# A fused two-block transformer kernel: sums moved to VectorE, a weight-difference loop in half the ticks, squares of one product set apart, a gate evacuation in parts

## The chip, the cores and the metric

The kernel runs on one core of one Trainium2 chip. A core has TensorE (PE, with its weight loads shown as PEld), VectorE (DVE), ScalarE (ACT), GpSimd (POOL) and SyncE (SP), which here issues all DMAs from one queue, in order. The metric is the device time of one execution in microseconds (us); lower is better.

## The reference, cut to what matters

A sequence of 1024 tokens of width 1024, in float32, passes through two blocks.

```python
# first block: dilated attention + RWKV-7 scan, merged by gates
h = rms_norm(x); proj = h @ w_in
y_attn = (o_attn * silu(z_attn)) @ w_up_attn
y_rwkv = (o_rwkv * silu(z_rwkv)) @ w_up_rwkv
merged = sigmoid(g_attn) * y_attn + sigmoid(g_rwkv) * y_rwkv
x = x + rms_norm(merged @ w_out)
# second block, first layer: gated spatial unit, 128-token chunks
u, v, z = split(rms_norm_2(x) @ a_w_in, 3)           # width 2048 each
s = W_causal @ layer_norm(gelu(v)) + b               # per chunk and group
x = x + rms_norm_2((gelu(u) * s * silu(z)) @ a_w_out)
# second block, second layer: sliding-window attention, 16 heads, 4 KV heads
q, z = split(rms_norm_2(x) @ b_w_in, 2)
out = x + rms_norm_2((attention(q, k, v) * silu(z)) @ b_w_out)
```

## The kernel before, in words

**Matmuls.** Every large product is made in three: weights and activations are split into a rounded high part (ACT: `whi`, `y_hi`, `Ahi`) and the rest (DVE: `wlo`, `y_lo`, `Alo`), and hi x hi, hi x lo and lo x hi are added up in a PSUM bank of 128 x 512. PSUM has two banks in pool `pd` and six in `pb`. SBUF tiles come from rings of slots: S2 (30 tiles of 128 x 512), S4 (19 of 128 x 1024) and A (8 of 128 x 2048). A slot goes to a new tile when the instructions and transfers of the old one are done; an instruction that writes the new tile waits for that.

**Order.** The order on each engine is the order in which the program emits instructions. Emission goes by ticks: `tick` (L166) is called after every four large matmuls and at the end of a group. A tick counts down the stores in `self.late` and issues those at the head of this list that are due (`store(dst, src, n)`, L157: n ticks later, four if nothing is said; the list is first in, first out), then loads and splits weights (`w_step`), then lets each lane go one step. A lane is a queue of generators; `yield n` means that the next part comes n ticks later. A `Bag` (such as `lane_n`) runs its generators side by side, a `Lane` one after the other. SP carries out its issues in the order of emission and stands still at a store whose source is not ready, so it runs ahead of the other engines until something holds it.

**Stages, in us of the profiled execution.** Up to 850: projections, and the RWKV scan beside them. 850 to 1160: dilated attention beside the rest of the projections (`phase1a`); in it `out_weights` (L1633) loads the four quadrants of a_w_out in eight row blocks, forms four differences on POOL (`minus`, tiles `tw`) and stores them in DRAM (`TW`). To 1440: the merge (`phase2`: gates loaded from `GT`, DVE's `m`) and the output product. 1440 to 1900: the second block's first layer (`phase3`): v, then for each of 16 column blocks the z and u products by a scheme of seven products (`seven`), with `vg` loaded for the spatial product. There `sums` (L2283) forms sums and differences of `y` that the output product wants, and stores them in `Y7`. 1913 to 2075: the output product a_out, itself in seven products (`run7`, L1976), each of four token tiles j; products n = 0 to 6, the sixth is n = 5. From the first half's results `norm` (L1935) makes residual, store of X2 and the next layer's normalised input, which PE transposes (`psT`). 2075 to 2505: the sliding-window attention (`phase4`) between projections, and the last output product. In `phase4` every z group is evacuated by `ev_z` (L2473): tanh on ACT, two products on DVE, the copy to `yb` on ACT, the difference on DVE. `att_norm` (L1092) divides the probabilities `P` on DVE before PE transposes them (L1122).

Of the kernel before, what the change touches and what calls it, by code (L numbers as in the profile page):

```python
# [9 lines left out]
F32 = mybir.dt.float32  # L10
F32R = mybir.dt.float32r
I32 = mybir.dt.int32
AF = mybir.ActivationFunctionType
# [1293 lines left out]
class Kernel(Attn):  # L1307
# [325 lines left out]
    def out_weights(self):  # L1633

        nc = self.nc
        W = self.I["a_w_out_2"][0]

        def load(r, c, k):
            t = self.s2("tw")
            nc.sync.dma_start(t, W[1024 * r + 128 * k:1024 * r + 128 * k + 128, 512 * c:512 * c + 512])  # L1640
            return t

        def minus(x, y, to, n, k):
            nc.gpsimd.tensor_tensor(out=to, in0=x, in1=y, op=ALU.subtract)
            if n is not None:
                self.store(self.TW[n][k], to, 4)

        for k in range(8):
            b11, b12, b22 = load(0, 0, k), load(0, 1, k), load(1, 1, k)
            yield 10  # L1650
            minus(b12, b11, b11, 0, k)
            yield 2
            minus(b22, b12, b12, 2, k)
            b21 = load(1, 0, k)
            yield 2
            minus(b22, b11, b22, 1, k)
            yield 6
            minus(b21, b22, b21, 3, k)
            yield 5

    def phase1a(self):
        self.att_setup()

        self.rw_pump(lambda: not self.lane_f.gens)
        self.lane_a.add(self.att_begin())
        self.lane_t = Lane(2)
        self.lane_a.add(self.att_tw())
        self.lanes = self.rw_lanes() + [self.lane_a, self.lane_m, self.lane_t]
        act = self.act_f
        i0 = self.first["pa"]  # L1670
        unit = lambda p, g: dict(p=p, g=g, L=T // DILATIONS[g], end=self.att_end1)
        A = self.lane_a
        us = {}

        def ahead(p, g):
            us[p, g] = unit(p, g)
            A.add(self.att_load(us[p, g]))

        def run(u):
            A.add(self.att_v(u))  # L1680
            A.add(self.att_unit(u))
        for n, x in enumerate(self.order_a):
            if type(x) is int:
                self.group(i0 + n, act, 8, 0, self.ev_g(self.GT[x - 57]))
                self.w_free(i0 + n)
                continue
            p, g, c = x
            dil = DILATIONS[g]
            if c == 2:
                while p > 1 and len(A.gens) > 7:  # L1690
                    for ln in self.lanes:
                        ln.step()
                u = unit(p, g)
            nm = ("q", "k", "vT")[c]
            u[nm] = self.s4(nm)
            ev = self.att_evac(u[nm], dil, 0.125 if c == 0 else None)
            for half in range(2):
                self.group(i0 + n, act, 8, half, ev)
            self.w_free(i0 + n)
            if c == 0:  # L1700
                u["bias"] = self.att_bias_load(g, p)
                ahead(p, 0)
                run(u)
                ahead(p, 1)
                run(us[p, 0])
                run(us[p, 1])
        self.lane_a.add(self.att_flush())
        i0 = self.first["pg"]
        self.gate_setup()
        for j, f in enumerate(self.order_g):  # L1710
            self.group(i0 + j, act, 8, 1, self.ev_g(self.GT[f - 57]))
            self.w_free(i0 + j)
# [145 lines left out]
    def out_proj(self, name, KT, post, xsrc, xdst, nxt, act):  # L1858
# [73 lines left out]
                nc.vector.scalar_tensor_tensor(out=x[:, s], in0=og[h], scalar=r, in1=x[:, s], op0=ALU.mult, op1=ALU.add)  # L1932
                nc.sync.dma_start(xdst[128 * tt:128 * tt + 128, s], x[:, s])

        def norm(half, og, x, ss, first=12, gap=3):  # L1935
            yield 2
            r = self.sm.tile([128, 4], F32, tag="or", name="or")
            st = self.sm.tile([128, 4], F32, tag="ost", name="ost")
            nc.vector.tensor_tensor(out=st, in0=ss[:, 0], in1=ss[:, 1], op=ALU.add)
            self.rms(st, r)  # L1940
            sv = self.sm.tile([128, 2, 4], F32, tag="osv", name="osv")
            for j in range(4):
                tt = 4 * half + j
                for h in range(2):
                    xs = x[j][:, 512 * h:512 * h + 512]
                    nc.vector.scalar_tensor_tensor(out=xs, in0=og[h, j], scalar=r[:, j:j + 1], in1=xs, op0=ALU.mult, op1=ALU.add)
                self.store(xdst[128 * tt:128 * tt + 128, :], x[j], 14 if nxt is not None else 0)
                yield 1
                if nxt is not None:
                    for h in range(2):  # L1950
                        nc.scalar.activation(out=og[h, j], in_=x[j][:, 512 * h:512 * h + 512], func=AF.Square,  # L1951
                                             accum_out=sv[:, h, j:j + 1])
            if nxt is None:
                return
            yield 2
            r2 = self.sm.tile([128, 4], F32, tag="or2", name="or2")
            nc.vector.tensor_tensor(out=st, in0=sv[:, 0], in1=sv[:, 1], op=ALU.add)
            self.rms(st, r2)

            def scaled(j):  # L1960
                for h in range(2):
                    xs = x[j][:, 512 * h:512 * h + 512]
                    if gnext is None:
                        nc.vector.tensor_scalar(out=og[h, j], in0=xs, scalar1=r2[:, j:j + 1], scalar2=None, op0=ALU.mult)
                    else:
                        nc.vector.scalar_tensor_tensor(out=og[h, j], in0=xs, scalar=r2[:, j:j + 1],
                                                       in1=gnext[:, 512 * h:512 * h + 512], op0=ALU.mult, op1=ALU.mult)
            scaled(0)
            for j in range(4):
                if j < 3:  # L1970
                    scaled(j + 1)
                yield gap if j else first
                yield from self.emit_T(lambda k: og[k // 4, j][:, 128 * (k % 4):128 * (k % 4) + 128], 4 * half + j, Ahi, Alo)
                self.act_done.add(4 * half + j)

        def run7(lanes, sums):  # L1976
# [24 lines left out]
            def evac(n, j, ps):  # L2001
                if n < 2:
                    t = (c1, c5)[n][j] = self.s2("og")
                    nc.scalar.copy(out=t, in_=ps)
                elif n == 2:
                    c2[j] = plus(ps, c1[j], self.s2("og"))
                elif n == 3:
                    out(0, 0, j, plus(ps, c1[j], c1[j]), nc.gpsimd)
                    u[j] = self.s2("og")
                    nc.gpsimd.tensor_tensor(out=u[j], in0=c2[j], in1=c5[j], op=add)  # L2010
                elif n == 4:
                    out(1, 0, j, plus(ps, u[j], u[j]), nc.vector)
                elif n == 5:
                    plus(ps, c2[j], c2[j])
                    nc.gpsimd.tensor_tensor(out=c5[j], in0=c2[j], in1=c5[j], op=add)
                    out(1, 1, j, c5[j], nc.gpsimd)
                else:
                    out(0, 1, j, plus(ps, c2[j], c2[j]), nc.vector)

            i0 = self.first[name]  # L2020
            for n in range(7):
# [20 lines left out]
                            evac(n, j, ps[j])  # L2042
                    self.w_free(i0 + 4 * n + kp)
                if n == 4:
                    self.lane_n.add(norm(0, og[0], x[0], ss[0], 18, 2))
            self.drain(self.lane_n)
            self.w_lim = 1000
            self.lane_n.add(norm(1, og[1], x[1], ss[1]))
# [178 lines left out]
    def phase3(self):  # L2227
# [55 lines left out]
        def sums(ct):  # L2283
# [2 lines left out]

            def do(x, y, op, n, to=None):
                t = self.s2("ysum") if to is None else to
                nc.gpsimd.tensor_tensor(out=t, in0=x, in1=y, op=op)
                self.store(self.Y7[n][c], t)  # L2290
                return t
            yield 4
            if ct < 8:
                do(ys[ct, 0], ys[ct, 1], ALU.subtract, 5)
                yield 2
# [129 lines left out]
    def phase4(self):  # L2425
# [38 lines left out]
                    self.group(self.first["bq"] + n, act, 8, 0, self.att_evac(qs[n], 1, 0.125))  # L2464
        self.Oh = {}
        yb = {}

        def end(u, Og):
            self.Oh[u["p"]] = Og

        def make_z(p):
            def ev_z(ps, half):
# [2 lines left out]
                s = slice(512 * half, 512 * half + 512)  # L2475
                t = self.s2("tz")
                nc.scalar.activation(out=t, in_=ps, func=AF.Tanh, scale=0.5)
                nc.vector.scalar_tensor_tensor(out=t, in0=t, scalar=1.0, in1=ps, op0=ALU.add, op1=ALU.mult)
                nc.vector.scalar_tensor_tensor(out=t, in0=t, scalar=0.5, in1=self.Oh[p][:, s], op0=ALU.mult, op1=ALU.mult)
                if p < 1:  # L2480
                    yb[p, half] = self.s2("yb_hi", F32R), self.s2("yb_lo", F32R)
                else:
                    y = self.s4("yb", F32R)
                    yb[p, half] = y[:, 0:512], y[:, 512:1024]
                self.split(t, *yb[p, half])
            return ev_z

        for n, c in enumerate(self.order_b):
            p = c % 8
# [5 lines left out]
            if c < 8:  # L2495
# [7 lines left out]
                self.lane_a.add(self.att_unit(u))  # L2503
                if p == 7:
                    self.lane_a.add(self.att_flush())
        self.flush()
        self.out3 = self.out_proj("b_out", 8, "b_post_g_2", self.X2, self.out, None, lambda k, half: yb[k, half])
        for half in range(2):
# [48 lines left out]
```

## Time and profile before

| | |
|---|---|
| median of 3 runs | 2505.64 us (2505.43 to 2506.14) |
| profiled execution | 2507.75 us, its span 2505.9 us |
| PE busy | 2418.4 us, 97% of the span |
| DVE, ACT, POOL busy | 1448.6, 1033.9, 832.8 us |
| mean granted clock of TensorE | 0.987 of full speed |

The span runs from the first to the last instruction. A matmul of 128 x 512 shows as some 0.39 us at full clock, but matmuls overlap, so PE's busy share counts time in which one was under way. A wait is put down to the instruction whose end released it.

### The profile page before, as it was taken

How to read it: one execution, taken by the hardware profiler on the slowest of the kernel's cores; microseconds unless marked ns; L12 is line 12 of the kernel's file. 1: busy time of each engine (PE TensorE's matmuls, PEld its weight loads, DVE VectorE, ACT ScalarE, POOL GpSimd, SP SyncE). 2: the span in 40 equal slices, each digit the busy share in tenths (PEclk: the TensorE clock that was granted, in tenths of full speed). 3: DMA queues.
4: the chain of work that ended last, by engine and by line, in shares of the span. 5: the costliest groups of instructions: out<-in, count | busy, mean ns of one | idle time of the engine just before them, and what ended most of it. 6: DMA issues, size and time to landing. Idle time of an engine off the chain costs nothing. (4 is left out here: it accounts for less than half of the span.)

```text
span 2505.9 us, 40000 instructions
## 1 busy us (share of the span) xinstructions
PE 2418.4 (97%) x14891; PEld 1904.7 (76%) x14891; DVE 1448.6 (58%) x3263; ACT 1033.9 (41%) x2539; POOL 832.8 (33%) x1055
## 2 busy tenths in 40 slices
PE   8999999999999999998899999999999988999998
PEld 6788777777777777776788778877777866777777
DVE  7764345554555355666747347556558666566545
ACT  4442232323232266553234223444445444566632
POOL 3443053434453012424500244656663122301000
PEclk8999999999999999999999999999999999999999
DMA  5334321212122346577733232333347743100033
GB/s 149 96 106 140 68 68 35 57 46 56 39 59 63 97 156 180 163 247 227 246 142 144 85 109 84 114 99 108 114 123 259 260 127 87 52 26 27 29 115 135
DMA packets 286263, 284.23 MB, mean 113 GB/s; under 512 B 27787, under 2 KB 208075, under 8 KB 286068
## 3 DMA queue, kind: packets, MB, share of 16 engines
q1 hardware_dynamic: 286068, 281.67, 36.3%
q8 instruction: 117, 1.92, 0.3%
q14 instruction: 78, 0.64, 0.1%
HBM read 206.87 MB, written 74.74 MB: 112 GB/s over the span
## 5 line engine op out<-in xcount | busy, mean ns | idle before, releaser
L349 PE MATMUL pd<-Ahi,whi 128*128 128x512 f32 x1232 | 497.4, 404 | 4.8 <-ACT whi L285 3.1
L349 PE MATMUL pd<-Ahi,wlo 128*128 128x512 f32 x1232 | 498.0, 404 | 4.0 <-DVE wlo L286 4.0
L349 PE MATMUL pd<-Alo,whi 128*128 128x512 f32 x1232 | 496.8, 403 | 1.4 <-DVE Alo L503 1.4
L286 DVE TENSOR_TENSOR wlo<-wraw,whi 128x512 fp32r<-128x512 f32 x348 | 279.6, 836 | 148.0 <-ACT whi L285 146.9
L349 PEld LDWEIGHTS pd<-Ahi,whi 128*128 128x128 f32 x1232 | 234.6, 190 | 57.7 <-ACT whi L285 3.7
L349 PEld LDWEIGHTS pd<-Alo,whi 128*128 128x128 f32 x1232 | 234.3, 190 | 55.1 <-issue 4.6
L349 PEld LDWEIGHTS pd<-Ahi,wlo 128*128 128x128 f32 x1232 | 234.3, 190 | 54.0 <-DVE wlo L286 5.8
L285 ACT ACTIVATE whi<-wraw 128x512 fp32r<-128x512 f32 x348 | 200.9, 621 | 36.9 <-DMA wraw<-in_b_w_out_dram 12.4
L1752 DVE TENSOR_TENSOR wlo<-wraw,whi 128x512 fp32r<-128x512 f32 x144 | 133.0, 934 | 81.1 <-ACT whi L1751 81.1
L1086 ACT ACTIVATE P<-P,ST 128x192 f32<-128x192 f32 (+2 forms) x320 | 130.5, 409 | 60.5 <-DVE ST L1074 57.3
L1751 ACT ACTIVATE whi<-wraw 128x512 fp32r<-128x512 f32 x144 | 89.5, 623 | 94.6 <-POOL wraw L228 91.7
L349 PE MATMUL pd<-wlo,Ahi 128*128 128x512 f32 x256 | 102.3, 400 | 5.2 <-DVE wlo L286 5.2
L799 POOL TENSOR_TENSOR X<-UC,X 128x60 f32<-128x60 f32 (+24 forms) x248 | 78.4, 316 | 82.8 <-DVE UC L792 64.4
L349 PE MATMUL pd<-whi,Ahi 128*128 128x512 f32 x256 | 101.4, 396 | 0.1
L349 PE MATMUL pd<-whi,Alo 128*128 128x512 f32 x256 | 101.3, 396 | 0.0
L228 POOL TENSOR_TENSOR wraw<-wraw 128x512 f32<-128x512 f32 x48 | 66.3, 1382 | 98.6 <-DVE wlo L1752 82.8
L278 POOL TENSOR_TENSOR wraw<-wraw,bpg 128x512 f32<-128x512 f32 x32 | 35.0, 1122 | 153.6 <-DMA wraw<-in_b_w_in_dram 141.5
L801 POOL TENSOR_TENSOR X<-X 128x60 f32<-128x60 f32 (+24 forms) x248 | 78.9, 318 | 19.4
L1157 PEld LDWEIGHTS psO<-PT,V 128*64 128x64 f32 x1040 | 55.6, 137 | 35.4 <-issue 18.2
L1157 PE MATMUL psO<-PT,V 128*64 128x128 f32 x1040 | 76.5, 284 | 5.1 <-DVE PT L1137 2.6
L1599 ACT ACTIVATE far<-pd 128x512 f32<-128x512 f32 x36 | 33.0, 917 | 101.9 <-PE pd L349 88.6
L2311 ACT ACTIVATE vg<-vg,lnv 128x128 f32<-128x128 f32 x128 | 53.4, 483 | 52.2 <-DMA vg<-Vd 51.7
(448 smaller groups left out, 5532.8 us busy)
## 6 DMA issues: line engine op xcount, KB each, us to landing
wraw<-in_w_in_dram SPq DMA_DIRECT2D x82, 512.0 KB
wraw<-in_a_w_in_dram SPq DMA_DIRECT2D x48, 512.0 KB
yraw<-Y SPq DMA_DIRECT2D x28, 512.0 KB
QD<-far SPq DMA_DIRECT2D x36, 256.0 KB
tw<-in_a_w_out_dram SPq DMA_DIRECT2D x32, 256.0 KB
TW<-tw SPq DMA_DIRECT2D x32, 256.0 KB
gate<-GT SPq DMA_DIRECT2D x32, 256.0 KB
wraw<-in_w_out_dram SPq DMA_DIRECT2D x16, 512.0 KB
```

Source lines behind the costliest of these rows:

```text
L228: nc.gpsimd.tensor_tensor(out=t[name], in0=t[x], in1=t[y], op=ALU.subtract)
L278: nc.gpsimd.tensor_tensor(out=t3[:, am], in0=t3[:, am], in1=gain[:, am].unsqueeze(2).to_broadcast([128, a // 2, b]), op=ALU.mult)
L285: nc.scalar.activation(out=his[j], in_=t[:, s], func=AF.Copy)
L286: nc.vector.tensor_tensor(out=los[j], in0=t[:, s], in1=his[j].bitcast(F32), op=ALU.subtract)
L349: nc.tensor.matmul(ps, lhsT=a, rhs=b, start=(n == 0), stop=(n == last))
L799: nc.gpsimd.tensor_tensor(out=tv, in0=U[:, j:j + 1, 0:j].to_broadcast([128, w, j]), in1=X[:, b0:8, j:j + 1].to_broadcast([128, w, j]), op= ...
L801: nc.gpsimd.tensor_tensor(out=X[:, b0:8, 0:j], in0=X[:, b0:8, 0:j], in1=tv, op=ALU.add)
L1086: nc.scalar.activation(out=it["P"][j][:, c], in_=Sx[j][:, c], func=AF.Exp, scale=-1.0, bias=ST[:, 0, n:n + 1], accum_out=ST[:, 1, n:n + 1])
L1157: nc.tensor.matmul(O(h).rearrange("p (s x) -> p s x", s=2), lhsT=V[:, b - 1 + t, c:c + 64], rhs=rhs, start=t == tiles[0], stop=t == 1)
L1751: nc.scalar.activation(out=hi, in_=src, func=AF.Copy)
L1752: nc.vector.tensor_tensor(out=lo, in0=src, in1=hi.bitcast(F32), op=ALU.subtract)
L2311: nc.scalar.activation(out=v[:, tt, :], in_=v[:, tt, :], func=AF.Identity, scale=lnv[:, tt, 1:2], bias=lnv[:, tt, 0:1])
```

## The change

Four places are changed. In `out_weights` all four loads of a row block come first, the subtractions follow at ticks 6, 7, 8 and 10, a block takes 12 ticks instead of 25, and a difference is stored 7 ticks after its subtraction instead of 4. `sums` works on VectorE instead of GpSimd, one tick sooner, and stores 8 ticks later instead of 4. In `run7` the squares (ACT) and scalings (GpSimd) of the sixth product leave its evacuation for a generator `last4`, which waits 6 ticks after the last tile and then does one tile per tick; the stores of X2 in the norm of the first half come 26 ticks after their sums instead of 14. In `phase4` the evacuation of a z group keeps only the tanh; the rest goes to a lane of its own in parts.

```diff
@@ out_weights
-                self.store(self.TW[n][k], to, 4)
+                self.store(self.TW[n][k], to, 7)
         for k in range(8):
             b11, b12, b22 = load(0, 0, k), load(0, 1, k), load(1, 1, k)
-            yield 10
+            b21 = load(1, 0, k)
+            yield 6
             minus(b12, b11, b11, 0, k)
+            yield 1
+            minus(b22, b12, b12, 2, k)
+            yield 1
+            minus(b22, b11, b22, 1, k)
             yield 2
-            minus(b22, b12, b12, 2, k)
-            b21 = load(1, 0, k)
+            minus(b21, b22, b21, 3, k)
             yield 2
-            minus(b22, b11, b22, 1, k)
-            yield 6
-            minus(b21, b22, b21, 3, k)
-            yield 5
@@ phase1a
-        self.lane_t = Lane(2)
+        self.lane_t = Lane(1)
@@ out_proj, norm
-        def norm(half, og, x, ss, first=12, gap=3):
+        def norm(half, og, x, ss, first=12, gap=3, late=14):
-                self.store(xdst[128 * tt:128 * tt + 128, :], x[j], 14 if nxt is not None else 0)
+                self.store(xdst[128 * tt:128 * tt + 128, :], x[j], late if nxt is not None else 0)
@@ out_proj, run7
                     nc.gpsimd.tensor_tensor(out=c5[j], in0=c2[j], in1=c5[j], op=add)
-                    out(1, 1, j, c5[j], nc.gpsimd)
+                    if j == 3:
+                        self.lane_n.add(last4())
+            def last4():
+                yield 6
+                for j in range(4):
+                    out(1, 1, j, c5[j], nc.gpsimd)
+                    yield 1
-                    self.lane_n.add(norm(0, og[0], x[0], ss[0], 18, 2))
+                    self.lane_n.add(norm(0, og[0], x[0], ss[0], 18, 2, 26))
@@ phase3, sums
-                nc.gpsimd.tensor_tensor(out=t, in0=x, in1=y, op=op)
-                self.store(self.Y7[n][c], t)
+                nc.vector.tensor_tensor(out=t, in0=x, in1=y, op=op)
+                self.store(self.Y7[n][c], t, 8)
-            yield 4
+            yield 3
@@ phase4
+        lane_z = Lane(1)
+        self.lanes.append(lane_z)
                 nc.scalar.activation(out=t, in_=ps, func=AF.Tanh, scale=0.5)
-                nc.vector.scalar_tensor_tensor(out=t, in0=t, scalar=1.0, in1=ps, op0=ALU.add, op1=ALU.mult)
-                nc.vector.scalar_tensor_tensor(out=t, in0=t, scalar=0.5, in1=self.Oh[p][:, s], op0=ALU.mult, op1=ALU.mult)
-                self.split(t, *yb[p, half])
+                lane_z.add(gate_z(ps, t, self.Oh[p][:, s], *yb[p, half]))
+        def gate_z(ps, t, o, h, l):
+            yield 1
+            nc.vector.scalar_tensor_tensor(out=t, in0=t, scalar=1.0, in1=ps, op0=ALU.add, op1=ALU.mult)
+            nc.vector.scalar_tensor_tensor(out=t, in0=t, scalar=0.5, in1=o, op0=ALU.mult, op1=ALU.mult)
+            yield 2
+            nc.scalar.activation(out=h, in_=t, func=AF.Copy)
+            yield 1
+            nc.vector.tensor_tensor(out=l, in0=t, in1=h.bitcast(F32), op=ALU.subtract)
+            yield 1
+        self.drain(lane_z)
         self.flush()
```

## Rows read from the trace of the kernel before

**Rows 1.** The page's busy table: busy us, share of the span, instructions.

```profile
PE 2418.4 (97%) x14891; PEld 1904.7 (76%) x14891; DVE 1448.6 (58%) x3263; ACT 1033.9 (41%) x2539; POOL 832.8 (33%) x1055
```

**Rows 2.** By stretch: length; busy us of PE, PEld, DVE, ACT, POOL; granted clock, DMA.

```profile
850.00:1105.00 255.00, 254.94 (x2169) 193.29 (x2167) 142.49 (x578) 144.27 (x509) 71.26 (x81) 1.00 0.59 179
1105.00:1230.00 125.00, 107.63 (x594) 83.58 (x591) 80.06 (x156) 40.28 (x107) 48.48 (x28) 0.95 0.78 247
...
1575.00:1900.00 325.00, 315.74 (x1477) 258.65 (x1476) 195.19 (x259) 151.22 (x315) 202.96 (x142) 0.99 0.39 118
...
2180.00:2400.00 220.00, 206.58 (x1608) 159.38 (x1608) 130.08 (x523) 142.21 (x516) 14.71 (x14) 0.98 0.09 28
```

**Rows 3.** The same view of four stretches behind gaps.

```profile
1112.00:1118.80 6.80, 4.53 (x24) 3.48 (x24) 4.27 (x16) 4.50 (x14) 0.00 (x0) 0.50 0.61 194
...
2054.10:2060.80 6.70, 3.83 (x11) 3.23 (x12) 6.70 (x8) 4.04 (x8) 5.56 (x5) 0.50 0.00 0
...
2204.30:2207.60 3.30, 3.30 (x10) 2.63 (x9) 2.91 (x17) 3.20 (x15) 0.00 (x0) 0.50 0.00 0
2388.60:2395.30 6.70, 4.47 (x14) 3.65 (x14) 5.02 (x16) 3.83 (x11) 0.00 (x0) 0.50 0.01 2
```

**Rows 4.** PE's waits: total us, times, longest us.

```profile
PE pb L1122 <- DVE P L1106: 12.8, 8, 4.2
PE pd L391 <- ACT vg L2311: 9.3, 5, 2.4
...
PE pd L349 <- DVE m L1777: 7.4, 4, 2.8
...
PE psT L499 <- DVE og L1998: 1.4, 1, 1.4
```

**Rows 5.** L1644 (ns, first and last start); timeline, ACT and PE: start, us.

```profile
L1644 POOL TENSOR_TENSOR tw<-tw x32: 1262/1290/1760, 876.6 to 1187.0; 128x512 f32<-128x512 f32 x32
...
1112.15 0.63 ACT L285 ACTIVATE whi<-wraw 128x512 fp32r<-128x512 f32 x1 [5.30 <-DMA TW<-tw]
...
1114.27 0.45 PE L1032 MATMUL pb<-K,vT 128*128 128x128 f32 x1 [4.28 <-DVE PT L1138]
```

**Rows 6.** Timeline of SP ahead of the first gate loads.

```profile
1163.73 2.96 SPq L1640 DMA_DIRECT2D tw<-in_a_w_out_dram  x3
1166.75 1.50 SPq L1768 DMA_DIRECT2D gate<-GT  x3
```

**Rows 7.** POOL busy with L2289; DVE group L2352 (mean ns); DVE's timeline near 1911.

```profile
1575.00:1930.00 355.00, 51.40 (x32) 0.99 0.42 131
...
L2352 DVE TENSOR_TENSOR y<-y,c 128x512 f32<-128x512 f32 x28 | 19.4, 693 | 30.1 <-POOL c L2346 30.1
...
1911.57 5.77 DVE L1752 TENSOR_TENSOR y_lo<-yraw,y_hi 128x512 fp32r<-128x512 f32 x4
```

**Rows 8.** Timeline of ACT and PE at the end of the sixth product.

```profile
2040.91 0.63 ACT L1993 ACTIVATE junk<-og 128x512 f32<-128x512 f32 x1 [7.32 <-POOL og L2015]
...
2052.25 0.63 ACT L1993 ACTIVATE junk<-og 128x512 f32<-128x512 f32 x1 [2.62 <-POOL og L2015]
...
2056.97 0.90 PE L499 MATMUL psT<-K,og 128*128 128x128 f32 x3 [6.14 <-DVE Alo L503]
```

**Rows 9.** SP's waits: total us, times, longest us.

```profile
SPq L172 <- DVE xr L1946: 153.5, 19, 39.7
```

**Rows 10.** Timeline of DVE at one gate evacuation; PE at three normalisations.

```profile
2190.59 0.69 DVE L2478 SCALAR_TENSOR_TENSOR tz<-tz,pd 128x512 f32<-128x512 f32 x1 [2.88 <-ACT tz L2477]
...
2193.31 0.15 DVE L1100 TENSOR_TENSOR es<-es,ST 128x4 f32<-128x4 f32 x1
...
2194.09 1.12 PE L1122 MATMUL pb<-K,P 128*128 128x128 f32 x6 [1.26 <-DVE P L1106]
...
2241.43 0.85 PE L1122 MATMUL pb<-K,P 128*128 128x128 f32 x4 [0.47 <-DVE P L1106]
...
2292.20 0.92 PE L1122 MATMUL pb<-K,P 128*128 128x128 f32 x5 [0.81 <-DVE P L1106]
```

## The prediction

> **What bounds the kernel now.** I read the busy table first [rows 1]: TensorE (PE) is busy for 97% of the span, and every other engine has at least 40% of it free. The table by stage comes next [rows 2]. In 850 to 1105 us PE waits for nothing (254.94 of 255.00). In the 125 us after that it loses 17.4 us, in the z/u stage (1575 to 1900) 9.3, and in the sliding-window attention (2180 to 2400) 13.4. So nothing that only makes another engine do less is worth anything: a gain has to come out of those few gaps, or out of the clock. Each larger gap is paid twice: behind some of them the granted clock is 0.50 for 3.3 to 6.8 us [rows 3], half of full speed (1.2 for 2.4 GHz), so such a dip costs half its length, 1.7 to 3.4 us. The list of PE's waits [rows 4] names who ends them: DVE's `P` (12.8 us in 8 waits), the `vg` scaling on ACT (9.3 in 5), DVE's `m` behind the gate loads (7.4 in 4), DVE's `og`.
>
> **The sum's base.** The profiled execution took 2507.75 us, its span 2505.9, and 1.85 lies around it. It stands 2.1 above the median of the three runs, 2505.64. I take differences from the trace and set them against the median.
>
> **Weight differences in half the ticks.** Nothing is added: 32 loads, 32 subtractions, 32 stores stay. A cycle of one row block goes from 25 ticks to 12, all four loads come first, and a store follows its subtraction by 7 ticks instead of 4. The 32 subtractions run from 876.6 to 1187.0 [rows 5], which is 7 x 25 + 20 = 195 ticks at 1.6 us; at 7 x 12 + 10 = 94 ticks they would end near 1026, before PE's losses begin. What leaves the later stretch: at 1112.15 ACT's `whi` had waited 5.30 us for a store of `tw` to land, because it writes into that tile's slot. PT and V copies queued behind it on ACT, and PE stood for 4.28 us [rows 5]. Behind that gap lies a dip of 6.80 [rows 3], so 4.28 + 3.40 = 7.7. Further on, three `tw` loads keep SP for 2.96 us right ahead of the first gate loads [rows 6], for which DVE's `m`, and then PE, wait; I take 1.5 of those 7.4 (bounds: nothing, and 3.0). Against it: 32 subtractions of 1.29 us and 16 MB of transfers are packed twice as densely, and from the loads to the issue of the stores the four tiles of a cycle hold S2 for 59 ticks in 12 instead of 60 in 25: 4.9 of its 30 slots instead of 2.4. SP's stores form one list in order, so a GT, SD or QD store behind a TW store now waits up to 3 ticks longer, and its source tile with it. PE waits for nothing there now, but the cover is not infinite: one stall like that of 1112 costs 7.7. I take 7.0 gained, between the bounds 0 and 10.7 and near the measured stall.
>
> **Sums of y on VectorE.** POOL gives up 32 instructions, 51.4 us [rows 7]. DVE gets 32; a like one, `y` by L2352, takes 693 ns [rows 7], so 22.2 us. The instructions of the two engines hold each other up: while POOL made three sums, four `y_lo` on DVE took 5.77 us instead of 4 x 0.69 = 2.8 [rows 7]. By "SBUF: two separate sides" in the Trainium skill's page "SBUF — State Buffer", a VectorE instruction with two SBUF inputs and a GpSimd one exclude each other for a whole instruction; the trace agrees with it, and by the rule alone 51.4 - 22.2 = 29.2 us of that pair would be won and the time come to some 2450. The PE waits don't bear such a gain: of this stretch they hold only the 9.3 us for `vg`, which ends with a transfer, and SP sends that transfer as soon as the weight loads ahead of it find a slot, not when a sum is ready. DVE is busy for 195 of 325 us there, which hides the 22.2. The stores wait 8 ticks instead of 4 and the first sum comes one tick sooner; SP stands behind the weight loads anyway. I take 0; bounds: -9.3, and +22.2 if all of it lies on the path.
>
> **Sixth product.** Now, for each of four token tiles, DVE adds, POOL adds (1.3 us), ACT squares, POOL scales. In ACT's queue the square stands ahead of the next `whi` and of `Ahi`: the first waited 7.32 us for POOL, the last came only at 2052.25 [rows 8], and behind it PE's transposes had stood for 6.14 us, after 1.40 for an `og` bank that DVE released late for the same reason [rows 4, 8]. Squares and scalings now go to a list of their own, 6 ticks later and one tile per tick, when POOL has made its four additions. Nothing is added, and og of this part is wanted only by the second norm, after the seventh product. 1.40 + 6.14 and half of the 6.70 us dip [rows 3] give 10.9; a short wait for a PSUM bank may be late next, so I take 9.5 (bounds 0 and 10.9). The four X2 stores of the first norm move 12 ticks later, past the weight loads behind them in SP's queue; such stores hold SP for 153.5 us in 19 waits [rows 9]. The loads behind are wanted well after, and the second norm's stores keep their 14 ticks: 0. The `xr` tiles stay 12 ticks longer in S4; that is 0 too, unless its 19 slots run short and SP's next weight load waits for one.
>
> **Gate evacuation.** Now ACT tanh, two DVE products, ACT copy and DVE difference follow each other in one tick: DVE is held from 2190.59 to 2193.31 (2.72 us, over half of it waiting), and the normalisation that PE's transposes L1122 need stands behind it; PE waited 1.26 [rows 10]. Eight waits make 12.8 [rows 4]; two of them (0.47, 0.81) have no gate ahead of them [rows 10], so six, 11.5 us, do. The parts come 1, 2 and 1 ticks apart now, so DVE waits for no ACT in them, and a normalisation that still falls behind a part stands behind 2 x 0.69 at most. 2.72 - 1.38 = 1.3 saved six times is 7.9. The two dips after these gaps cost (3.3 + 6.7) / 2 = 5.0, of which I take half. From 10.4 I take off 0.9 for parts that fall ahead of a normalisation that was free before: 9.5 (bounds 3 and 16.5). PSUM is held about two ticks longer, and a bank comes round again after two groups of six ticks.
>
> **Sum.** 7.0 + 0 + 9.5 + 9.5 = 26.0: 2505.64 - 26.0 = 2479.6, say 2480 (2481.8 against the profiled execution).
>
> **Rivals.** (1) The denser weight differences crowd S2 and SP's list, and the stall of 1112 comes in 850 to 1105 instead. One costs 7.7; with four (30.8) the whole gain is gone, with all eight cycles it is 61.6 and the time 2541. For it: that stall is one of exactly this kind. Against: it came when the gated tiles shared S2 too, and PE waits nowhere before. 6 in 100, slower. (2) The gate parts only move the collision to other normalisations: the 9.5 go, 2489. 11 in 100. (3) The sums on DVE come on the path, through late evacuations L405 or late `wlo`: +22.2, 2502, no measurable change. Against: no PE wait names them now. 7 in 100. (4) With POOL lighter the `vg` waits go too: -9.3, 2470. 8 in 100. The forecast keeps 68.
>
> **How the numbers follow.** The forecast's own range is 2468 to 2490 (weight differences 3 to 10, sixth product 6.5 to 10.9, gates 6 to 16.5). From 2466 to 2494 it takes in rival 2 and most of rival 4, and leaves out 1 and 3 and a few of the rest, under 2 in 10. Within 0.2% (5 us, about what a measurement can tell from no change) lies only rival 3: 0.07; slower is rival 1: 0.06; faster the rest: 0.87.
>
> **What would show it.** Right: no PE wait for the PT copy near 1110 and no dip there, the last subtraction before 1050; no wait of transposes for `Alo` over 1 us near the end of the sixth product; PE's waits for `P` in the attention at 5 us or less. Wrong: PE waits in 850 to 1050, ACT's `whi` waiting for TW stores there; PE waiting for DVE's `c` in the z/u stage; `P` waits still at 10 us.

## The result and the profile after

The changed kernel takes 2465.76 us (median of four runs, 2463.28 to 2469.01) against 2505.89 for the kernel before: ratio 0.9841, interval [0.9823, 0.9858], 40.1 us less. The forecast was 2480 (26.0 less), its range 2466 to 2494: the direction was right, and the time lies at the very edge of the range, 0.2 us under its lower end as written.

The page's busy table of the changed kernel (to be read against [rows 1]):

```profile
PE 2407.2 (98%) x14891; PEld 1899.8 (77%) x14891; DVE 1451.9 (59%) x3295; ACT 1033.3 (42%) x2539; POOL 793.4 (32%) x1023
```

POOL has 32 instructions fewer and DVE 32 more, as the diff says; PE has the same 14891, in a span that is 42.8 us shorter: 11.2 less of PE's busy time and 31.6 less of its idle time. The table by stretch of the changed kernel (length; busy us of PE, PEld, DVE, ACT, POOL; granted clock, DMA share, GB/s), each moved by about what had been gained ahead of it:

```profile
850.00:1105.00 255.00, 255.00 (x2168) 193.51 (x2167) 139.30 (x576) 142.89 (x505) 83.51 (x92) 1.00 0.64 201
1100.00:1220.00 120.00, 109.92 (x645) 85.66 (x644) 84.86 (x180) 43.95 (x121) 37.59 (x20) 0.97 0.69 217
1560.00:1880.00 320.00, 315.98 (x1497) 259.56 (x1496) 203.33 (x296) 153.24 (x319) 164.77 (x114) 1.00 0.41 123
2150.00:2370.00 220.00, 214.17 (x1660) 166.62 (x1657) 137.87 (x531) 143.41 (x517) 13.14 (x12) 1.00 0.11 32
```

Against [rows 2]: 850 to 1105 is still without a gap, though POOL does 12 us more in it. PE's idle time falls from 17.4 us in 125 to 10.1 in 120, from 9.3 to 4.0 in the z/u stage, and from 13.4 to 5.8 in the attention. PE's waits of the changed kernel (total us, times, longest us; against [rows 4]):

```profile
PE pd L349 <- DVE m L1777: 5.5, 3, 2.1
PE pb L1122 <- DVE P L1106: 5.2, 4, 3.0
PE pd L391 <- ACT vg L2318: 4.0, 5, 1.4
PE psO L1157 <- DVE PT L1137: 3.4, 1, 3.4
```

Both kernels issue the same matmuls in the same order, so the n-th of one trace can be set against the n-th of the other. By the time given (of the kernel before), the changed kernel is ahead by 9.4 us at 1200, 11.5 at 1460, 22.2 at 1920, 31.1 at 2060, 30.8 at 2180 and 42.9 at 2400. So the stages of the four edits gave about 9.4, 10.7, 8.9 and 12.1 (the first counts from the kernel's start; at 1100 the changed kernel was 1.6 behind). The forecast had 7.0, 0, 9.5 and 9.5: it left out the z/u stage. These are differences of two single executions: in the kernels below, stages that an edit doesn't touch move by up to 4 us (`sixth_late` is 4.4 behind at 850, ahead of its edit). Sizes are therefore taken from timed ratios.

### The profile page after: what moved, and what is told of

It reads as the page before. It is cut to its first block, busy times and chain, and to the rows that moved or that the text cites. A ratio compares the mean times of both kernels' runs of the same rounds, so it can differ in the third digit from the quotient of the medians.

```text
span 2463.1 us, 40015 instructions
## 1 busy us (share of the span) xinstructions
PE 2407.2 (98%) x14891; PEld 1899.8 (77%) x14891; DVE 1451.9 (59%) x3295; ACT 1033.3 (42%) x2539; POOL 793.4 (32%) x1023
## 4 chain that ended last, share of the span: by engine, by line
PE 84%; DVE 6%; DMA 4%; ACT 3%; issue 2%; SPq 0%; POOL 0%; DVEq 0%; ACTq 0%; POOLq 0%
PE pd L349 39%; PE pd L391 8%; PE psP L391 8%; PE pb L2044 4%; PE pb L1884 4%; PE pd L1884 3%; PE psO L1157 2%; PE pb L1056 2%; PE pb L1122 2%; DMA vg<-Vd 1%; PE pb L349 1%; PE pd L2044 1%; DVE wlo L286 1%; PE pb L2338 1%; PE pb L743 1%
## 5 line engine op out<-in xcount | busy, mean ns | idle before, releaser
L286 DVE TENSOR_TENSOR wlo<-wraw,whi 128x512 fp32r<-128x512 f32 x348 | 278.7, 832 | 143.2 <-ACT whi L285 142.5
L1752 DVE TENSOR_TENSOR wlo<-wraw,whi 128x512 fp32r<-128x512 f32 x144 | 120.7, 849 | 81.3 <-ACT whi L1751 81.3
L228 POOL TENSOR_TENSOR wraw<-wraw 128x512 f32<-128x512 f32 x48 | 71.6, 1492 | 98.6 <-DVE wlo L1752 86.0
```

The source lines that it names most:

```text
L286: nc.vector.tensor_tensor(out=los[j], in0=t[:, s], in1=his[j].bitcast(F32), op=ALU.subtract)
L1752: nc.vector.tensor_tensor(out=lo, in0=src, in1=hi.bitcast(F32), op=ALU.subtract)
```

## The experiments

Each kernel was timed in turn with the kernel before on the same chip; the kernel before had medians of 2506.9 to 2508.4 us there.

**The parts one by one.** Four kernels have one of the four edits each; together they are the changed kernel.

```diff
only_sums:     -  nc.gpsimd.tensor_tensor(out=t, in0=x, in1=y, op=op)
               -  self.store(self.Y7[n][c], t)              # and yield 4
               +  nc.vector.tensor_tensor(out=t, in0=x, in1=y, op=op)
               +  self.store(self.Y7[n][c], t, 8)           # and yield 3
only_weights:  the hunks out_weights and phase1a alone
only_sixth:    the hunks of norm and run7 alone (late=26, last4)
only_gate:     the hunks around gate_z and lane_z alone
```

`only_sums`: 

> Only the sums of y change: engine, store delay 8 instead of 4, first yield 3 instead of 4. Theory A (the traces of before and after aligned at the same matmuls): the z/u stage ends about 10 us earlier, because the loads of vg land earlier against TensorE and two half-clock stretches go; 2495 to 2498. Theory B (the forecast's term for this part): nothing, 2505 to 2507, with five vg waits of 9 us still there. Theory C: VectorE's added 22 us show in part, over 2508.

`only_weights`: 

> Only the weight differences change (order, yields, store delay 7, lane step 1). Theory A (alignment of the traces): 9 us less by 1200 us of the span, 2496 to 2497. Theory B (forecast): 7.0 less, 2499. Theory C: the gain at 1110 was made by something else in the change and the trace near 1440 is lost again here: 2503 or more.

`only_sixth`: 

> Only the sixth product changes: squares and products of its four tiles in a generator of their own, and the first norm's stores held 26 ticks instead of 14. Theory A (alignment): 8 to 9 less, 2497. Theory B (forecast): 9.5 less, 2496. Theory C: the later stores take back part at the second norm, 2501 or more.

`only_gate`: 

> Only the gate evacuation changes, one part per tick. Theory A (alignment): 12 less, 2494, waits of TensorE for P at most 6 us in the last 220 us. Theory B (forecast): 9.5 less, 2496. Theory C: the waits for P were not made by the gate parts and move: 2503 or more.

| kernel | median us | ratio to before, interval | gain at 2507.7 us |
|---|---|---|---|
| only_sums | 2498.93 | 0.9967 [0.9956, 0.9979] | 8.3 |
| only_weights | 2497.79 | 0.9965 [0.9952, 0.9978] | 8.8 |
| only_sixth | 2498.63 | 0.9967 [0.9957, 0.9978] | 8.3 |
| only_gate | 2494.79 | 0.9957 [0.9945, 0.9970] | 10.8 |

The gains are (1 - ratio) x 2507.7, each uncertain by about 3 us; they add to 36.2 beside the 40.1 of the whole, a difference within these uncertainties, so no large effect of two edits together shows. Theory B falls for the sums, whose interval (5.3 to 11.0) excludes 0. For the other three, theories A and B lie at most 3 us apart, and the times don't tell them from each other; `only_sums` and `only_sixth` came out some 1 to 2 us above theory A. Theory C (added work that shows, or a gain that is lost again) falls in all four.

**Why the sums gain: engine or store delay.**

```diff
sums_engine:  -  nc.gpsimd.tensor_tensor(out=t, in0=x, in1=y, op=op)
              +  nc.vector.tensor_tensor(out=t, in0=x, in1=y, op=op)
sums_lag:     -  self.store(self.Y7[n][c], t)
              +  self.store(self.Y7[n][c], t, 8)            # and yield 4 -> 3
```

`sums_engine`: 

> The kernel before with the sums of y on VectorE and nothing else (stores 4 ticks later, first yield 4, as before). Theory A (it is the engine: POOL's queue is shorter, so the weight differences that free the slots come sooner and the load of vg behind the weight loads on SP's queue goes out sooner): the gain of the whole part, ratio 0.996 to 0.998, 2496 to 2500 beside 2506. Theory B (it is the store delay: SP's queue waits less on the sums before the load of vg): less than a third of it, 2503 to 2506.

`sums_lag`: 

> The kernel before with the sums of y still on POOL, their stores 8 ticks later instead of 4 and the first yield 3 instead of 4. Theory A (engine): within 3 us of the kernel before, vg waits of TensorE still 8 to 10 us. Theory B (store delay): 6 to 9 us faster, vg waits at about 4 us.

Measured: `sums_engine` 2496.57 us, 0.9966 [0.9954, 0.9979], the whole gain; `sums_lag` 2507.52 us, 0.9998 [0.9990, 1.0007], none. It is the engine. In 1575 to 1900, first PE's waits and a group of DVE's instructions (ns min/median/max, first and last start) in `sums_lag`, then in `sums_engine`:

```profile
PE pd L391 <- ACT vg L2311: 8.7, 6, 2.3
```

```profile
L1752 DVE TENSOR_TENSOR wlo<-wT,whi x14: 1172/1176/1186, 1581.0 to 1875.3; 128x512 fp32r<-128x512 f32 x14
```

```profile
PE pd L391 <- ACT vg L2311: 3.4, 4, 1.2
```

```profile
L1752 DVE TENSOR_TENSOR wlo<-wT,whi x14: 674/675/676, 1585.3 to 1872.8; 128x512 fp32r<-128x512 f32 x14
```

All 14 of these splits took 0.50 us longer with the sums on POOL. One of them in the kernel before, DVE's row and POOL's (timeline: start, us), starts while POOL makes a sum, which itself took 1.74 us. Whether these splits are the ones that cost time is taken up further on.

```profile
1715.37 1.18 DVE L1752 TENSOR_TENSOR wlo<-wT,whi 128x512 fp32r<-128x512 f32 x1
```

```profile
1714.26 1.74 POOL L2289 TENSOR_TENSOR ysum<-y 128x512 f32<-128x512 f32 x1
```

**Does the `vg` load stand behind the weight loads?** The forecast had it there, and held that a sum can't matter to it.

```diff
vg_act:   -  nc.sync.dma_start(v, Vd[:, :, 128 * ct:128 * ct + 128]...)
          +  nc.scalar.dma_start(v, Vd[:, :, 128 * ct:128 * ct + 128]...)
```

`vg_act`: 

> The kernel before, sums of y on POOL as they were, but the loads of vg issued from ScalarE's queue instead of SP's, so that they don't stand behind weight loads that wait 13 us for slots. Theory A (the late issue and landing of vg set the pace of the z/u stage, and the sums on POOL only made them later): vg waits of TensorE below 4 us instead of 9.3, 2497 to 2502. Theory B (SP's wait is not what makes vg late: the slot comes free no sooner, and the transfer of 6 to 7 us is the time): 2505 to 2510, waits as before. Theory C (the issue holds ScalarE up): over 2510.

Measured: 2493.08 us, 0.9942 [0.9928, 0.9956], so 14.5 us less, more than theory A expected. PE waits for nothing in the z/u stage, though POOL has its sums:

```profile
1575.00:1900.00 325.00, 325.00 (x1543) 268.85 (x1542) 221.97 (x279) 161.08 (x331) 214.84 (x148) 1.00 0.41 127
```

One load in the kernel before (timelines of SP, then of ACT) and the same one in `vg_act` (ACT, then SP):

```profile
1711.03 0.38 SPq L209 DMA_DIRECT2D wraw<-in_a_w_in_dram  x1
...
1712.09 0.42 SPq L209 DMA_DIRECT2D wraw<-in_a_w_in_dram  x1
1712.62 1.06 SPq L2308 DMA_DIRECT2D vg<-Vd  x1
```

```profile
1720.04 0.88 ACT L2311 ACTIVATE vg<-vg,lnv 128x128 f32<-128x128 f32 x2 [5.07 <-DMA vg<-Vd]
```

```profile
1696.82 0.37 ACTq L2308 DMA_DIRECT2D vg<-Vd  x1
...
1704.71 0.86 ACT L2311 ACTIVATE vg<-vg,lnv 128x128 f32<-128x128 f32 x2
```

```profile
1700.90 0.38 SPq L209 DMA_DIRECT2D wraw<-in_a_w_in_dram  x1
```

The load now goes out 4.1 us ahead of the weight load, not 1.6 behind the first of two, and ACT finds its data there. The matmul that waited 2.34 us in the kernel before starts there at 1724.44, and its counterpart in `vg_act` at 1718.28 without a wait, so the load is issued 21.5 us ahead of it instead of 11.8. The tile was free by then: theory B falls. The instruction itself takes ACT's queue 0.37 us (theory C falls). The 9.3 us of waits and half of two dips of 3.3 us, 12.6 together, lie within the timed gain (11.0 to 18.1).

**Sixth product: the list apart, or the later stores.** `sixth_late` has `late=26` alone, `sixth_apart` has `last4` alone.

```diff
sixth_late:   -  self.lane_n.add(norm(0, og[0], x[0], ss[0], 18, 2))
              +  self.lane_n.add(norm(0, og[0], x[0], ss[0], 18, 2, 26))
sixth_apart:  -  out(1, 1, j, c5[j], nc.gpsimd)
              +  if j == 3:
              +      self.lane_n.add(last4())
```

`sixth_late`: 

> The kernel before with the first norm's stores held 26 ticks instead of 14, squares and products not moved. Forecast's step (the long queue of additions and squares on VectorE and POOL at the end of the sixth product delays the split Alo): the wait of 6.1 us for Alo stays, gain at most 2 us, 2504 to 2507. Rival (SP's queue, blocked on the first norm's stores, is what is late): the gain of the whole part, 2497 to 2499.

`sixth_apart`: 

> The kernel before with squares and products of the sixth product's tiles in a generator of their own, the first norm's stores at 14 ticks as before. Forecast's step: the gain of the whole part, 2496 to 2499, no wait for Alo over 1 us at the end of the sixth product. Rival: 2504 to 2507.

Measured: `sixth_late` 2508.35 us, 1.0005 [0.9995, 1.0014]; `sixth_apart` 2497.51 us, 0.9961 [0.9948, 0.9973]. The later stores are worth nothing here, and the list apart is the whole part. PE's waits in 1980 to 2140 of `sixth_late`, then of `sixth_apart`:

```profile
PE psT L499 <- DVE Alo L503: 6.1, 1, 6.1
PE pd L349 <- DVE wlo L286: 3.8, 1, 3.8
```

```profile
PE pd L349 <- DVE wlo L286: 3.3, 1, 3.3
PE pd L349 <- ACT Ahi L502: 2.3, 2, 1.9
```

**Weight differences: the order, or the early end.** The order, the stores and the lane of the change, but 25 ticks for a block as before.

```diff
weights_slow:  yields of a block 6, 1, 1, 2, 2  ->  13, 2, 2, 4, 4
```

`weights_slow`: 

> The weight differences in the order of the change, with all four loads up front, stores 7 ticks later and a lane step of 1, but with 25 ticks for each of the eight groups as in the kernel before instead of 12. Theory A (forecast: it is the early end that takes the wait for a TW store out of 1105 to 1130): no gain, 2505 to 2509, the last subtraction after 1150 and a wait of 3 us or more near 1110. Theory B (the order and the early fourth load make the gain): most of the 9 us, 2497 to 2500.

Measured: 2510.73 us, 1.0013 [1.0002, 1.0024]: no gain, if anything a small loss. The order and the early fourth load are not what pays. Its subtractions (ns, first and last start) and PE's waits in 1090 to 1225:

```profile
L1644 POOL TENSOR_TENSOR tw<-tw x32: 1261/1288/1747, 877.4 to 1187.1; 128x512 f32<-128x512 f32 x32
```

```profile
PE pd L349 <- DVE m L1777: 9.7, 4, 4.5
PE psO L1157 <- DVE PT L1138: 3.2, 2, 2.0
PE psO L1157 <- DVE PT L1137: 2.8, 1, 2.8
PE pb L1032 <- DVE PT L1138: 1.5, 1, 1.5
PE pb L1122 <- ACT V L1037: 1.4, 1, 1.4
PE pb L1056 <- DVE ST L1074: 1.2, 1, 1.2
```

The same waits in `only_weights`, whose subtractions end early:

```profile
PE psO L1157 <- DVE PT L1137: 3.4, 1, 3.4
PE pd L349 <- DVE m L1777: 3.3, 1, 3.3
PE psO L1157 <- DVE PT L1138: 1.6, 1, 1.6
```

That is 19.8 us against 8.3. Yet the single wait of 4 us near 1110 that theory A expected is not in `weights_slow`: three of 1.2 to 1.5 us stand in its place (1112.8 to 1119.4), none of them behind a TW store.

**Gate evacuation: the delay, or the spreading.** `gate_z` as in the change, but all four parts in the tick after the tanh.

```diff
gate_delay:  -      yield 2      # ahead of ScalarE's copy
             -      yield 1      # ahead of VectorE's difference
```

`gate_delay`: 

> The gate evacuation one tick after its tanh, but all four parts in that one tick instead of one part per tick. Theory A (spreading: VectorE's three gate instructions of 0.7 us in a row stand ahead of the P evacuation): a third to half of the gain is left, 2500 to 2504, P waits of 7 to 11 us. Theory B (delay: VectorE no longer stands behind the tanh of the same tick): nearly the whole gain, 2494 to 2498, P waits of 5 to 6 us.

Measured: 2502.59 us, 0.9982 [0.9973, 0.9991], 4.5 us of the 10.8. PE's waits for `P` in the attention of `gate_delay`, then of `only_gate`:

```profile
PE pb L1122 <- DVE P L1106: 9.8, 6, 4.3
```

```profile
PE pb L1122 <- DVE P L1106: 4.9, 4, 3.0
```

Theory A holds: about two fifths of the gain come with the delay by one tick, the rest with spreading the parts. That the delay pays because DVE no longer stands at the tanh of the same tick is argued; no run shows it by itself.

**The changed kernel with `vg` on ScalarE's queue.** The edit of `vg_act`, made to the changed kernel.

`after_vg_act`: 

> The changed kernel with the loads of vg issued from ScalarE's queue as well. Theory A (the sums on VectorE and the vg loads on ScalarE's queue take away the same waits, of which the changed kernel still has 4.0 us in five): no vg waits of TensorE left, 4 to 6 us less than the changed kernel, ratio to the kernel before 0.9815 to 0.983. Theory B (the two gains are separate and add up, 0.33 and 0.58%): 14 us less, ratio 0.9785 or below. Theory C (the change left nothing to gain there): 0.984.

Measured: 2463.67 us, 0.9825 [0.9812, 0.9839]. No wait for `vg` is left:

```profile
1575.00:1900.00 325.00, 325.00 (x1535) 268.67 (x1534) 217.57 (x313) 161.67 (x331) 157.96 (x109) 1.00 0.44 139
```

Theory B falls: a ratio of 0.9785 lies outside the interval, so the two edits mostly take away the same waits. That this version beats the changed kernel (0.9841 [0.9823, 0.9858]) the times don't settle, since the intervals overlap; in the traces it loses 4.0 us less to `vg`.

## Why the prediction was right, and where it was short

**Total.** The range holds the result only to its rounding, and that is in part luck. The forecast's own range ended at 2468; 2466 was drawn to take in most of a rival held at 8 in 100. Three of the four terms came out within their uncertainty, the fourth was put at nothing, and the 3.9 by which the whole exceeds the sum of the parts pushes the same way.

**Bound.** Right: the gain came out of PE's gaps and the clock, and VectorE's 32 added instructions cost nothing that shows (DVE is busy for 203 of 320 us of the z/u stage).

**Weight differences: 7.0 forecast, 8.8 measured [5.5 to 12.0].** The end near 1026 came out at 1019 (ns, first and last start, in the changed kernel):

```profile
L1644 POOL TENSOR_TENSOR tw<-tw x32: 1272/1290/1742, 878.3 to 1018.8; 128x512 f32<-128x512 f32 x32
```

Nothing moved into 850 to 1105, so rival 1 did not come. Waits for `m` behind the gate loads fell from 7.4 to 5.5: the 1.5 was fair. The mechanism was too narrow. With the store wait taken as the cause, `weights_slow` should have kept one stall of its kind; it had others of about that sum. What they share is that subtractions and their transfers still run beside the gates and the attention's last units; whether POOL, the queue of SP or the slots carries that on was not separated. And one wait is left that the early end does not touch (it was 2.57 us in the kernel before, at 1130.16), now with a half-clock stretch of 3.4 us behind it. In the changed kernel's timeline (DVE, then PE), the mixing weights' reciprocal and two splits stand ahead of `PT`:

```profile
1122.93 0.94 DVE L1273 RECIPROCAL mws<-mws 16x128 f32<-16x128 f32 x1
...
1124.38 0.67 DVE L1728 TENSOR_TENSOR or_lo<-oa,or_hi 128x512 fp32r<-128x512 f32 x1
1124.98 0.67 DVE L286 TENSOR_TENSOR wlo<-wraw,whi 128x512 fp32r<-128x512 f32 x1
1125.68 0.29 DVE L1137 COPY PT<-pb 64x128 f32<-64x128 f32 x1
```

```profile
1126.03 0.48 PE L1157 MATMUL psO<-PT,V 128*64 128x128 f32 x4 [3.35 <-DVE PT L1137]
```

**Sums on VectorE: 0 forecast, 8.3 measured [5.3 to 11.0].** This is the step that failed, and rival 4, held at 8 in 100, came in part: more than half of the `vg` waits went, and the clock with them. The sentence was that SP sends the `vg` transfer "as soon as the weight loads ahead of it find a slot, not when a sum is ready". The first half is right, and `vg_act` shows it. The second half stopped one link early. The slot comes free with DVE's split `wlo` (SP's waits in 1575 to 1900 of the kernel before, total us, times, longest us):

```profile
SPq L209 <- DVE wlo L1752: 200.1, 20, 14.6
```

When that split comes depends on POOL's queue some 10 us earlier. In the kernel before, ahead of the `vg` load of 1712.62 (DVE, then POOL):

```profile
1697.57 1.12 DVE L2364 SCALAR_TENSOR_TENSOR tz<-tz,c 128x512 f32<-128x512 f32 x1 [2.61 <-ACT tz L2363]
1698.61 1.78 DVE L1752 TENSOR_TENSOR wlo<-wraw,whi 128x512 fp32r<-128x512 f32 x1
...
1700.91 1.39 DVE L1752 TENSOR_TENSOR wlo<-wraw,whi 128x512 fp32r<-128x512 f32 x1
```

```profile
1695.58 1.30 POOL L2289 TENSOR_TENSOR ysum<-y,ysum 128x512 f32<-128x512 f32 x1
...
1698.09 1.75 POOL L228 TENSOR_TENSOR wraw<-wraw 128x512 f32<-128x512 f32 x1
1700.46 1.29 POOL L228 TENSOR_TENSOR wraw<-wraw,wT 128x512 f32<-128x512 f32 x1 [0.63 <-DVE wlo L1752]
```

The same place of the changed kernel (DVE, then POOL):

```profile
1683.10 0.68 DVE L1752 TENSOR_TENSOR wlo<-wraw,whi 128x512 fp32r<-128x512 f32 x1
...
1685.07 0.70 DVE L1752 TENSOR_TENSOR wlo<-wraw,whi 128x512 fp32r<-128x512 f32 x1 [0.69 <-ACT whi L1751]
```

```profile
1680.60 1.74 POOL L228 TENSOR_TENSOR wraw<-wraw 128x512 f32<-128x512 f32 x1
1683.93 1.30 POOL L228 TENSOR_TENSOR wraw<-wraw,wT 128x512 f32<-128x512 f32 x1 [1.58 <-DVE wlo L1752]
```

The sums push POOL's weight differences back (the first starts 24.0 us ahead of the PE wait at 1722.10, in the changed kernel 26.1 us ahead of the same wait, at 1706.74), so that they run beside these two splits. From there each step waits for the one before it: DVE's sum `c`, ACT on `c`, POOL's product, DVE's `y`, then such a round once more, and at last the split whose end lets SP go on at 1711.03. Measured from the start of that wait, the first of the two splits starts 23.5 and 23.6 us ahead, the second ends 19.8 and 21.0 ahead, and `vg` is issued 9.5 ahead before and 10.7 in the changed kernel; it lands 0.7 us sooner after that, which is not explained, and the wait falls from 2.34 to 0.47 us. The pair took 1.77 to 1.79 and 1.39 to 1.40 us ahead of all four waits of about 2 us in the kernel before, and 0.68 to 0.70 ahead of all five waits of the changed kernel. So a sum on POOL reaches SP after all. The 14 splits of `wT`, 0.50 us longer each, are not the way here: behind such a split DVE stands for 2.61 us until ACT's `tz`, which takes up the 0.50. This is read from traces; no timed run parts POOL's order from the longer instructions. The price given to rival 4 was near: waits fell from 9.3 to 4.0, and two half-clock stretches of 3.3 us, worth 1.65 each, went with them: 8.6.

The rule of the Trainium skill ("SBUF — State Buffer", "SBUF: two separate sides") agrees with the stretching (1.78 us beside POOL's difference, 0.68 without); what it was worth to the time was not 29.2 us, but what lay on the way to `vg`.

**Sixth product: 9.5 forecast, 8.3 measured [5.5 to 10.8].** Right, and the 0 for the later stores too (`sixth_late`). The terms are another matter. The waits of 1.40 and 6.14 went, but the half of the dip did not: the changed kernel has two dips of 3.4 us at 2010 and 2048 in the place of one of 6.8 at 2054, while short waits for weights (`whi`, `wlo`) fell by 2.4. These fell by 2.2 in `sixth_late` too, which gains nothing, so what made up for the dips is not shown. The table by stretch of the changed kernel:

```profile
2010.30:2013.70 3.40, 3.40 (x10) 2.62 (x9) 3.10 (x13) 2.06 (x4) 0.00 (x0) 0.51 1.21 295
2047.90:2051.30 3.40, 3.40 (x9) 2.63 (x10) 2.34 (x11) 0.72 (x2) 0.00 (x0) 0.50 0.00 0
```

The dip of 2054 was also overpriced: PE worked in only 3.83 of its 6.70 us [rows 3], so by half of that it cost 1.9, not 3.4. The same holds for 1112 (4.53 of 6.80) and 2388 (4.47 of 6.70). The two dips at 2010 and 2048, with PE busy throughout, cost 3.4 in the same way.

**Gate evacuation: 9.5 forecast, 10.8 measured [7.5 to 13.8].** Right; rival 2, that the collision only moves, fell. Waits for `P` went from 12.8 in eight to 5.2 in four (just over the 5 that was the line drawn), 7.6 less; of the four, one (1.08 us) still has gate parts in the 4.5 us ahead of it, and the longest (2.98) has none. One reading was wrong: of DVE's 2.72 us it waited not for over half, but for some 0.7, nearly all of it here:

```profile
2192.70 0.69 DVE L1752 TENSOR_TENSOR yb_lo<-tz,yb_hi 128x512 fp32r<-128x512 f32 x1 [0.69 <-ACT yb_hi L1751]
```

The 1.3 us taken for each of six waits is thus half waiting and half the difference, which is now a part of its own; the 7.9 they give is near the 7.6. Both half-clock dips after such waits are gone in `only_gate` and in the changed kernel; by PE's busy time in them [rows 3] they cost (3.3 + 4.47) / 2 = 3.9, and 7.6 + 3.9 = 11.5. The forecast took half of 5.0 for them, and that is the term that was short.

## What to carry to other kernels

When an edit relieves an engine whose name stands in no wait, follow the wait that is there back link by link, past the DMA queue to what frees the slot of the load ahead, before costing the edit at nothing. A load that is wanted soon and stands on an in-order queue behind loads that wait for slots can be issued from another engine's queue: here that was worth 14.5 us, and moving the sums off the chain behind the slots 8.3. An evacuation of several dependent parts on two engines was cheaper here spread over ticks (10.8 us gained) than merely delayed (4.5).

## What the hardware showed that was not expected

- A split of `wT` on VectorE took 1.18 us with the sums on POOL and 0.675 without, in all 14 cases, and these cost no time that the trace shows; two other splits, beside POOL's weight differences (1.78 and 1.39 us instead of 0.68 and 0.70), were the ones on the way.
- The `vg` load, 512 KB, took 0.37 us of ScalarE's queue each time in `vg_act`; on SP's queue the same instruction took 0.36 to 2.12 us in the kernel before.
- A half-clock stretch that follows a gap can begin before PE is back at work (at 2054.10, PE's next matmul at 2056.97). By estimate it costs half of PE's busy time in it (1.9 us there), not half of its length (3.4).
